# Position products of a Fourier layer, tied behind products of an output tile

## The chip, the cores and the metric

The kernel runs on one core of one Trainium2 chip. The metric is the device time of one execution in microseconds (us); three runs of the kernel before gave a median of 1564.77 us (1563.36 to 1567.52). TensorE (PE) multiplies matrices and transposes, VectorE (DVE) does elementwise work and the low parts of operands, ScalarE (ACT) copies, casts and takes activations, GpSimd (POOL) and SyncE (SP) do little but start transfers in the part of the kernel that matters here.

## The reference

Two residual layers and a final norm, on a prompt of 2048 positions and a sample of 512, 1024 channels each:

```python
def fourier_layer(x, g, w_gate, w_out):
    b, s, d = x.shape
    h = rmsnorm(x, g)
    hg = h.astype(jnp.float32).reshape(b, s, N_FGROUPS, FGROUP_CH)
    f = jnp.fft.fftn(hg, axes=(1, 3), norm="ortho").real
    f = f.reshape(b, s, d).astype(x.dtype)
    gate = h @ w_gate
    return x + (f * jax.nn.silu(gate)) @ w_out

def trunk(x, ...):
    x = attention_layer(x, ...)   # windowed attention, |i-j| <= 128
    x = fourier_layer(x, ...)
    return rmsnorm(x, final_norm)
```

The change lies in the Fourier layer, in the transform over positions of the prompt.

## The kernel before, in words

Every product of float32 matrices is made of three products of high and low parts (`matmul3`, line 131): high times high, high times low, low times high. To make the parts of an operand, ACT casts the high part and DVE subtracts it for the low part; where the text speaks of a split, it means this pair.

The Fourier layer first takes the transform over channels, tile by tile (128 positions), and combines the 16 tiles of the prompt in groups of four (`radix4`). The combined tiles ("spectra") of three groups go to DRAM (`evd`, `odd`), those of the last group stay in SBUF (`kept`). What follows runs position class by position class: `k1` from 0 to 8 stands for the output positions k1 + 16 j, and for their mirror 16 - k1 + 16 j where there is one.

For each class DVE builds one or two spectra `G[k1]` out of the loaded tiles by sums and differences (`pm`, line 2039, gives a sum in a new tile and the difference in place; `tt` is one such operation, 1024 columns, line 1502). Then `position` (line 1677) does the following. It loads the gate rows and the table of cosines and sines (`position_loads`, line 1656: SP, or POOL for mirrored rows, and POOL for the table). It takes buffers for one or two output tiles `up` with `zt`. For each half of the columns it splits the spectra (`halves_of`, line 1659: ACT L1668, DVE L1669, tiles `gp`), multiplies them by the table on PE into a pair of PSUM banks (`acc` inside `position`, tiles `ABp`: 6 products for a half of class 0 or 8, 12 for a half of the others, so 24 in each step below), and combines the two banks into `up` (ACT copies L1702 and L1705, DVE sums L1706 to L1709). At the end DVE multiplies `up` by the gate rows (L1712). PSUM has two pairs of banks for `ABp` and for the turns below.

`turned` (line 1242) transposes an `up` tile on PE (`tw`, 16 transposes, L112) and splits the result into `tTu`. `finish` (line 1745) is the output projection of such a tile: two halves of the columns, for each 8 blocks k of three products, so 48 products `fo`; DVE adds the result to the residual rows (L1759), then come the final norm (ACT L1261, DVE L127, POOL L128, DVE L1729) and the store (SP L1731).

`step` (line 1940) puts these together: the products of the new positions, the projection of the oldest waiting tile, the turns of the new tiles, the projection of the next waiting tile. The steps of the part that changes are:

- `emit(0, 8)`: classes 0 and 8, while the last two tiles of the sample (`pend`) are projected; all its spectra come from `w0`, four tiles of which three are loaded (`ev`)
- `emit(4)`: class 4, from the differences of `w0`
- `emit(2)`: class 2, from `w2`
- class 6, written out by hand: its `position`, eight loads of sums of the output weights (`f_sums("T1")`, `f_sums("T2")`, tiles `fT`), the projection of the first tile of class 2, the first half of the second tile's, the turns of class 6 (inside `o.operands`), the second half.

The order in which the engines get their work is that of a planner: each engine takes instructions from a queue in a fixed order, which the planner makes from the program's order as a priority, from its own estimate of durations, and from the buffers that are free. Tiles of one tag share a number of buffers: `right` (and so `zt`) has 16, `hT` has 8 (operands of PE), `x` has 4 (residual and gate rows). `after(ins, anchor)` (line 190) ties an instruction behind another in the queue, with no wait of its own; `matmul3` takes it as `behind`. In the kernel before, the turns are tied behind the projected tile and behind the last position product (`chain["turns"]`, `chain["B"]`), the next projection behind the turns. The position products themselves are not tied.

Of the kernel before, what the change touches and what calls it, by code (L numbers as in the profile page):

```python
# [25 lines left out]
KD = D // P  # L26
# [24 lines left out]
def f32(ap):  # L51
    return ap.bitcast(F32)
# [3 lines left out]
def encoder(  # L56
# [74 lines left out]
    def matmul3(out, a, b, start, stop, more=False, behind=None):  # L131

        for i, j in ((0, 0), (0, 1), (1, 0)):
            ins = pe(PE.matmul(out, a[i], b[j], start=start and i + j == 0, stop=stop and i == 1, skip_group_check=more))  # L134
            after(ins, behind)
        return ins
# [64 lines left out]
    def pe(ins):  # L201
        return seq(PE, ins) if PE in chain else ins
# [1013 lines left out]
    def fourier_phase(tail):  # L1216
        with ExitStack() as es:
# [9 lines left out]
            def right(shape, dtype, name):  # L1227
                return zp.tile(shape, dtype, align_bytes=LINE, tag="R", bufs=16, name=name)
# [3 lines left out]
            def zt(name):  # L1232
                return right([P, D], F32, name)
# [267 lines left out]
            def tt(out, a, b, op):  # L1501
                DVE.tensor_tensor(out, a, b, op)
# [38 lines left out]
            for i, s in enumerate(tail):  # L1541
# [7 lines left out]
                if 1 <= i < 9:  # L1549
                    w, k = split_steps[i - 1]  # L1550
# [105 lines left out]
            def position_loads(name, tab, tiles):  # L1656
                return [gated(name, r, xtile) for r in tiles], table(name, tab, left)

            def halves_of(name, gr, gs, hf, after_one=None):

                out = []
                for i, g in enumerate((gr, gs)):
                    if i and after_one:
                        after_one()
                    if g is not None:
                        t = main.tile([P, 2, 512], F32R, align_bytes=LINE, tag="hT", bufs=8, name=f"g{name}_{hf}_{i}")
                        gv = g[hf] if isinstance(g, list) else g[:, hf * 512 : hf * 512 + 512]
                        ACT.copy(t[:, 0], gv)  # L1668
                        low = DVE.tensor_tensor(t[:, 1], gv, f32(t[:, 0]), ALU.subtract)  # L1669
                        if chain.get("steps"):  # L1670
                            seq("dve", low)
                        out.append(t)
                return out
# [3 lines left out]
            def position(name, tab, gr, gs, tiles, loads=None, parts=None, between=None, later=None):  # L1677

                s2s, tb = loads or position_loads(name, tab, tiles)
                cs, sn, ns = [(tb[:, 2 * i], tb[:, 2 * i + 1]) for i in range(3)]  # L1680
                us = [zt(f"u{name}_{i}") for i in range(len(tiles))]
                for hf in range(2):
                    if hf and between:
                        between()
                    ts = parts[hf] if parts and parts[hf] else halves_of(name, gr, gs, hf)

                    def acc(out, tabs, c0, n):
                        for i, (w, t) in enumerate(zip(tabs, ts)):
                            v = [
                                t[:, part].rearrange("p (g c) -> p g c", g=2)[:, :, c0 : c0 + n]  # L1690
                                for part in range(2)
                            ]
                            end = matmul3(out, w, v, i == 0, i == len(ts) - 1)
                        return end

                    ab = two_banks(f"AB{name}_{hf}")
                    a, b = ab[:, 0, :260], ab[:, 1, :256]
                    a, b = (t.rearrange("p (g c) -> p g c", g=2) for t in (a, b))
                    chain["A"] = acc(a, (cs, ns), 0, 130)
                    chain["B"] = acc(b, (sn, cs), P, P)  # L1700
                    uv = [u.rearrange("p (g c) -> p g c", g=4)[:, 2 * hf : 2 * hf + 2] for u in us]
                    ACT.copy(uv[0][:, :, 0 : P + 1], a[:, :, 0 : P + 1])  # L1702
                    re, im = uv[0][:, :, 1:P], b[:, :, 1:P]
                    for v in uv[1:]:
                        ACT.copy(v[:, :, 0 : P + 1 : P], a[:, :, 0 : P + 1 : P])  # L1705
                        DVE.tensor_tensor(v[:, :, 1:P], re, im, ALU.add)  # L1706
                        DVE.tensor_tensor(v[:, :, P + 1 : 256], re, im, ALU.subtract)
                    DVE.tensor_tensor(uv[0][:, :, P + 1 : 256], re, im, ALU.add)
                    last_b[0] = DVE.tensor_tensor(re, re, im, ALU.subtract)  # L1709
                for u, s2 in zip(us, s2s):  # L1710
                    if later is None:
                        gated_by.append(DVE.tensor_tensor(u, u, s2, ALU.mult))  # L1712
                    else:
                        later.append(lambda u=u, s2=s2: after(DVE.tensor_tensor(u, u, s2, ALU.mult), last_c[0]))
                return list(zip(us, tiles))
# [26 lines left out]

            late = [None]

            def finish(uT, r, between=None):
                r0 = r[0]
                x2 = residual(r)
                for half in range(2):
                    if half and between:
                        chain["turns"] = end  # L1750
                        between()
                    ps = psum2.tile([P, 512], F32, tag="acc", name=f"fo{r0}_{half}")
                    for k in range(KD):
                        first_one = k == 0 and half == (between is not None)
                        end = matmul3(
                            ps, uT[k], wo[half * KD + k], k == 0, k == KD - 1, behind=chain.get("turns") if first_one else None
                        )
                    xs = x2[:, half * 512 : half * 512 + 512]
                    DVE.tensor_tensor(xs, xs, ps, ALU.add)  # L1759
# [172 lines left out]
            def pair(k1, R, base):  # L1932

                if k1 == 0 or 2 * k1 == R:
                    return [(base + k1, R, None)]
                return [(base + k1, R, None), (base + R - k1, R, k1 if R == 16 else 0)]

            pend = []

            def step(*positions):  # L1940
                new = [t for p in positions for t in position(*p)]
                if pend:
                    end = finish(*pend.pop(0))
# [70 lines left out]
            new = position(*early[0])  # L2014
# [8 lines left out]
            new = turned_one + turned(new[1:])  # L2023
# [22 lines left out]
            def emit(*ks):  # L2046
                step(*((f"p{k1}", k1, *G[k1], pair(k1, 16, 0)) for k1 in ks))

            e, g4r = pm(w0[0], w0[2], "e0")
            f, g4s = pm(w0[1], w0[3], "f0")  # L2050
            r0, r8 = pm(e, f, "r0")
            G[0], G[8], G[4] = (r0, None), (r8, None), (g4r, g4s)
            emit(0, 8)
            c2 = math.sqrt(0.5)
            sm, df = pm(w2[1], w2[3], "sm")
            g2r = zt("g2r")
# [3 lines left out]
            DVE.scalar_tensor_tensor(g2s, sm, c2, w2[2], ALU.mult, A)  # L2060
            DVE.scalar_tensor_tensor(w2[2], sm, c2, w2[2], ALU.mult, S)
            G[2], G[6] = (g2r, g2s), (w2[0], w2[2])
            emit(4)
            pc, qs = [], []
            for a in range(4):
                for i, l in enumerate((pc, qs)):
# [3 lines left out]
                    t = zt(f"od{a}_{i}")  # L2070
# [3 lines left out]
            for a in range(1, 4):  # L2074
# [6 lines left out]
                DVE.scalar_tensor_tensor(qs[a], qs[a], ca, tmp, ALU.mult, A)  # L2081
                tcs.append(c_)
                tsn.append(qs[a])
            emit(2)
            e0c, e1c = pm(tcs[0], tcs[2], "e0c")
            o0c, o1c = pm(tcs[1], tcs[3], "o0c")
            e0s, e1s = pm(tsn[0], tsn[2], "e0s")
# [15 lines left out]
            p6 = [halves_of("p6", *G[6], 0), None]  # L2103
# [5 lines left out]
            for k1 in (3, 5):  # L2109
                for t, g in zip(god[k1], G[k1]):  # L2110
                    ACT.dma_start(t, g)
            o = Outs(6, position("p6", 6, *G[6], pair(6, 16, 0), None, p6))
            f_sums("T1", right)
            f_sums("T2", right)
            finish(*pend.pop(0))
            finish(*pend.pop(0), o.operands)
            o.others()
            o.load()
# [17 lines left out]
            for k1, k2 in ((1, 7), (7, 3), (3, 5), (5, None)):  # L2136
# [30 lines left out]
                o = nxt["o"]  # L2167
# [108 lines left out]
```

## Time and profile before

| | |
|---|---|
| median of 3 runs | 1564.77 us |
| profiled execution, its own time | 1567.89 us |
| its span | 1566.1 us |
| PE busy | 1545.2 us (99%) |
| DVE busy | 1123.7 us (72%) |
| ACT busy | 889.5 us (57%) |
| POOL busy | 450.7 us (29%) |
| DMA | 237 GB/s over the span |

In a line of the timeline the columns are start and duration in us, engine, line of the program, operation, output and inputs by the program's names, shapes, and how many instructions the line merges; in brackets stands how long the engine was idle before it and what ended that. The start of a merged line is that of its first instruction. Matmuls overlap, so the durations of a group add up to a little more than the time from its start to the next group. In a table of stretches, the pairs are busy time and count for PE, PEld, DVE, ACT and POOL, then follow the granted share of TensorE's clock, the busy share of the DMA engines and GB/s. In a list of waits stand the total in us, how often, and the longest.

### The profile page before, as it was taken

Reading aid. Unit: us, or ns where it says so; the run is one execution under the profiler, and the core shown is the slowest. Engines: PE = TensorE matmul, PEld = TensorE weight load, DVE = VectorE, ACT = ScalarE, POOL = GpSimd, SP = SyncE. Lnnn points to the kernel's source line nnn. Section 1 sums busy time; section 2 is a strip of 40 time slices with the busy share of each in tenths; the row PEclk is TensorE's granted clock in tenths of the full one; section 3 lists DMA queues with packets and bytes.
Section 4 is the critical chain, followed back from the end, with each engine's and each line's share of the span. In section 5 each row is a group of like instructions: output and inputs, shape, how many; then the busy total and the mean of one; then the engine's idle time right before and its main releaser. Section 6 shows DMA issues by size and latency. Waiting matters only on the chain.

```text
span 1566.1 us, 33658 instructions
## 1 busy us (share of the span) xinstructions
PE 1545.2 (99%) x13150; PEld 1350.9 (86%) x13150; DVE 1123.7 (72%) x2431; ACT 889.5 (57%) x1921; POOL 450.7 (29%) x616
## 2 busy tenths in 40 slices
PE   9999999999999999999999999999999999899998
PEld 7899888999898888988888899988888888788886
DVE  5888655777637776367764577767888877889896
ACT  6788534787337784257861477746656554333353
POOL 2565662421414313314214142222112111101100
PEclk9999999999999999999999999999999999999999
DMA  9677687684856765866749666675666679456852
GB/s 330 232 264 234 222 336 280 216 293 161 297 218 220 243 232 204 302 210 205 251 136 363 232 206 224 243 257 181 223 234 218 220 242 409 149 202 250 298 191 94
DMA packets 100729, 372.70 MB, mean 238 GB/s; under 512 B 11235, under 2 KB 22251, under 8 KB 83420
## 3 DMA queue, kind: packets, MB, share of 16 engines
q1 hardware_dynamic: 82716, 297.38, 54.8%
q0 software_dynamic: 16688, 70.04, 11.5%
q10 hardware_dynamic: 1168, 3.15, 0.6%
q8 instruction: 103, 1.69, 0.4%
q14 instruction: 54, 0.44, 0.1%
HBM read 280.06 MB, written 90.47 MB: 237 GB/s over the span
## 4 chain that ended last, share of the span: by engine, by line
PE 88%; DVE 6%; DMA 3%; ACT 2%; issue 1%; POOL 0%; POOLq 0%; ACTq 0%; DVEq 0%; SPq 0%
PE pj L524 27%; PE av L750 7%; PE W L134 6%; PE pj L134 6%; PE tp L134 5%; PE av L134 5%; PE spt L650 5%; PE spt L134 4%; PE tp L709 3%; PE Wo L134 3%; PE fo L134 3%; PE Z L134 3%; PE z L1385 2%; PE Zo L134 2%; PE ABp L134 2%; PE X L134 1%
## 5 line engine op out<-in xcount | busy, mean ns | idle before, releaser
L524 PE MATMUL pj<-h,wg 64*128 64x512 f32 x1920 | 440.3, 390 | 0.0
L524 PE MATMUL pj<-h,wq 64*128 64x512 f32 x1560 | 380.4, 390 | 1.3 <-DVE qab L568 1.3
L524 PEld LDWEIGHTS pj<-h,wg 64*128 64x128 f32 x1920 | 331.5, 185 | 22.6
L524 PEld LDWEIGHTS pj<-h,wq 64*128 64x128 f32 x1560 | 285.4, 185 | 22.9 <-DVE qab L568 2.7
L669 DVE CUSTOM_DVE_ANT_0 S<-spt,b 128x385 f32<-128x385 f32 (+1 forms) x320 | 165.0, 525 | 94.1 <-PE spt L650 89.7
L677 ACT ACTIVATE S<-S 128x385 f32<-128x385 f32 (+1 forms) x320 | 189.2, 592 | 62.1 <-DVE S L669 40.5
L722 ACT CAST pts<-tp 128x768 fp32r<-128x768 f32 (+1 forms) x160 | 121.3, 758 | 96.6 <-PE av L750 59.8
L726 DVE TENSOR_TENSOR pts<-tp,pts 128x768 fp32r<-128x768 f32 (+1 forms) x160 | 144.1, 901 | 14.1 <-ACT pts L722 13.4
L750 PE MATMUL av<-pts,v 64*128 64x256 f32 x1680 | 143.7, 287 | 3.0 <-DVE pts L726 3.0
L750 PEld LDWEIGHTS av<-pts,v 64*128 64x128 f32 x1680 | 127.3, 186 | 7.3 <-DVE pts L726 3.8
L795 POOL TENSOR_TENSOR uT<-o,uT 128x256 fp32r<-128x256 f32 x75 | 56.7, 756 | 244.5 <-ACT uT L791 244.2
L650 PE MATMUL spt<-kwin,qab 64*128 64x384 f32 (+1 forms) x960 | 121.4, 339 | 0.9 <-DVE S L669 0.7
L134 PE MATMUL fo<-wo,tTu 128*128 128x512 f32 x480 | 115.7, 395 | 0.0
L134 PEld LDWEIGHTS fo<-wo,tTu 128*128 128x128 f32 x480 | 89.4, 190 | 18.1
L709 PEld LDWEIGHTS tp<-ident,S 64*128 64x128 f32 x1792 | 93.1, 137 | 10.1 <-DVE pts L726 3.1
L709 PE MATMUL tp<-ident,S 64*128 64x64 f32 x1792 | 98.0, 224 | 0.1
L786 POOL TENSOR_TENSOR o<-o,s 128x256 f32<-128x256 f32 x75 | 55.6, 742 | 120.3 <-DVE o L780 95.0
L692 DVE TENSOR_SCALAR S<-S 128x384 f32<-128x384 f32 (+1 forms) x192 | 88.5, 489 | 0.1
L650 PEld LDWEIGHTS spt<-kwin,qab 64*128 64x128 f32 x960 | 85.1, 188 | 3.8 <-issue 1.8
L279 DVE SCALAR_TENSOR_TENSOR h<-xk,g0s,h 128x512 fp32r<-128x512 f32 x40 | 45.3, 1146 | 51.3 <-ACT h L278 51.1
L524 PE MATMUL pj<-wo,uT 64*128 64x512 f32 x360 | 74.8, 390 | 0.0
L278 ACT ACTIVATE h<-xk,g0s 128x512 fp32r<-128x512 f32 x40 | 28.7, 724 | 75.2 <-POOL xk L274 75.1
(376 smaller groups left out, 3355.8 us busy)
## 6 DMA issues: line engine op xcount, KB each, us to landing
wo<-wsd SPq DMA_DIRECT2D x32, 1024.0 KB, 5.9
wq<-wsd SPq DMA_DIRECT2D x31, 1024.0 KB, 6.5
wg<-wsd SPq DMA_DIRECT2D x31, 1024.0 KB, 5.8
x<-x1d SPq DMA_DIRECT2D x40, 512.0 KB, 3.8
b<-b21d SPq DMA_DIRECT2D x40, 512.0 KB, 4.7
b<-rowd SPq DMA_DIRECT2D x40, 384.0 KB, 4.2
xs<-in_x_dram SPq DMA_DIRECT2D x23, 512.0 KB, 6.2
s2d<-gt POOLq DMA_DIRECT2D x40, 256.0 KB, 4.2
```

The costliest lines, as they stand in the source:

```text
L134: ins = pe(PE.matmul(out, a[i], b[j], start=start and i + j == 0, stop=stop and i == 1, skip_group_check=more))
L524: out.last[h] = pe(PE.matmul(out.ps, a[i], b[j], **out.flags()))
L650: pe(PE.matmul(spt[j][:, 2 + k0 * P : 2 + k1 * P], res["q"][rows, qp, b * P : (b + 1) * P], kwin[g][rows, kp, b * P + k0 * P : b * P + k1 ...
L669: seq(DVE, DVE.tensor_tensor_reduce(out=s[:, e0:e1], in0=ps[:, 1 + e0 : 1 + e1], in1=st["bias"][:, j, 386 - e1 : 386 - e0][:, ::-1], scale ...
L677: last_exp[0] = seq(ACT, ACT.activation(s[:, e0:e1], s[:, e0:e1], AF.Exp, bias=s[:, 386:387], scale=-1.0, accum_out=s[:, 387:388]))
L692: seq(DVE, DVE.tensor_scalar(s[:, ks], s[:, ks], den, None, ALU.mult))
L709: pe(PE.transpose(ps[h][:, kb, j, :], s[rows, j, 1 + kb * P : 1 + (kb + 1) * P], ident[rows, rows]))
L722: seq(ACT, ACT.copy(hi, ps))
L726: seq(DVE, DVE.tensor_tensor(lo, ps, f32(hi), ALU.subtract))
L750: last[i][h] = pe(PE.matmul(av[:, i, :256], v[rows], pt[rows], start=not swap and n == 0, stop=swap and n == len(todo[h]) - 1, skip_group_ ...
L786: eng.tensor_tensor(o, o, s, ALU.mult)
L795: low = eng.tensor_tensor(lo, o, f32(hi), ALU.subtract)
```

## The change

Position products can now be tied behind products of the tile that is being projected. `finish` takes a function `within` and a number `n`: after block n of its 16 (3 n products) it remembers the last product in `chain["rows"]` and calls `within`, which traces the positions; `acc` passes that product as `behind`. `step` takes the number first: 10 for classes 0 and 8 (30 products), 0 for class 4 (not tied, positions first, as before), 3 for class 2 (9 products). Before the projection starts, `step` does the loads of all its positions and the split of the first half of the first one. For class 6 the number is 10; its loads stay ahead of all, the eight loads of `f_sums` now stand ahead of its products and of its `up` tiles.

The differences of `w0` (`g4r`, `g4s`, the spectra of class 4) stood ahead of classes 0 and 8 in the program; they now stand behind that step.

```diff
-                            end = matmul3(out, w, v, i == 0, i == len(ts) - 1)
+                            end = matmul3(out, w, v, i == 0, i == len(ts) - 1, behind=chain.get("rows"))
...
-            def finish(uT, r, between=None):
+            def finish(uT, r, between=None, within=None, n=0):
...
+                        if within and half * KD + k + 1 == n:
+                            chain["rows"] = end
+                            within()
+                            chain.pop("rows")
...
-            def step(*positions):
-                new = [t for p in positions for t in position(*p)]
-                if pend:
-                    end = finish(*pend.pop(0))
+            def step(n, *positions):
+                new, held = [], []
+                for i, p in enumerate(positions):
+                    held.append((position_loads(p[0], p[1], p[4]), None if i else [halves_of(p[0], p[2], p[3], 0), None]))
+
+                def within():
+                    for p, h in zip(positions, held):
+                        new.extend(position(*p, *h))
+
+                if not n:
+                    within()
+                end = finish(*pend.pop(0), None, within, n)
...
-            e, g4r = pm(w0[0], w0[2], "e0")
-            f, g4s = pm(w0[1], w0[3], "f0")
+            e, f = zt("e0"), zt("f0")
+            for n, a, b in ((e, 0, 2), (f, 1, 3)):
+                tt(n, w0[a], w0[b], A)
             r0, r8 = pm(e, f, "r0")
-            G[0], G[8], G[4] = (r0, None), (r8, None), (g4r, g4s)
-            emit(0, 8)
+            G[0], G[8], G[4] = (r0, None), (r8, None), (w0[0], w0[1])
+            emit(10, 0, 8)
+            for a in range(2):
+                tt(w0[a], w0[a], w0[a + 2], S)
...
-            emit(4)
+            emit(0, 4)
...
-            emit(2)
+            emit(3, 2)
...
-            o = Outs(6, position("p6", 6, *G[6], pair(6, 16, 0), None, p6))
+            six = []
+            at6 = position_loads("p6", 6, pair(6, 16, 0))
             f_sums("T1", right)
             f_sums("T2", right)
-            finish(*pend.pop(0))
+            finish(
+                *pend.pop(0), None,
+                lambda: six.append(Outs(6, position("p6", 6, *G[6], pair(6, 16, 0), at6, p6))), 10,
+            )
+            o = six[0]
             finish(*pend.pop(0), o.operands)
```

More of the change, by code (lines that the diff above doesn't have):

```diff
@@ L2044, in pm, with emit @@
                 return n, a
-            def emit(*ks):
-                step(*((f"p{k1}", k1, *G[k1], pair(k1, 16, 0)) for k1 in ks))
-            e, g4r = pm(w0[0], w0[2], "e0")
-            f, g4s = pm(w0[1], w0[3], "f0")
+            def emit(n, *ks):
+                step(n, *((f"p{k1}", k1, *G[k1], pair(k1, 16, 0)) for k1 in ks))
+            e, f = zt("e0"), zt("f0")
+            for n, a, b in ((e, 0, 2), (f, 1, 3)):
+                tt(n, w0[a], w0[b], A)
             r0, r8 = pm(e, f, "r0")
-            G[0], G[8], G[4] = (r0, None), (r8, None), (g4r, g4s)
-            emit(0, 8)
+            G[0], G[8], G[4] = (r0, None), (r8, None), (w0[0], w0[1])
+            emit(10, 0, 8)
+            for a in range(2):
+                tt(w0[a], w0[a], w0[a + 2], S)
             c2 = math.sqrt(0.5)
```

## The prediction

> **What bounds the kernel now.** I read the page's busy times, then TensorE's waits late in the run, then granted clock and busy times by stretch, then the timeline of TensorE and of the engines that feed it.
>
> ```profile
> span 1566.1 us, 33658 instructions
> ...
> PE 1545.2 (99%) x13150; PEld 1350.9 (86%) x13150; DVE 1123.7 (72%) x2431; ACT 889.5 (57%) x1921; POOL 450.7 (29%) x616
> ```
>
> TensorE (PE) is the bound: 20.9 us of the span are not PE. No product is added or removed, so the change can only move waits of PE. From 1318 to 1450 us, where all edits lie, the waits are:
>
> ```profile
> PE ABp L134 <- ACT gp L1668: 4.3, 1, 4.3
> ...
> PE ABp L134 <- DVE gp L1669: 1.0, 2, 0.8
> ```
>
> and the stretches around the long one (PE, PEld, DVE, ACT, POOL busy; PEclk is the granted clock):
>
> ```profile
> 1334.37:1338.70 4.33, 0.00 (x1) 0.00 (x0) 4.33 (x7) 0.67 (x2) 0.00 (x0) 0.79 0.41 146
> 1338.70:1346.00 7.30, 7.30 (x28) 6.30 (x29) 5.30 (x10) 3.31 (x7) 1.45 (x2) 0.66 0.39 136
> ```
>
> PE stands for 4.33 us, and afterwards runs at 0.66 of its clock for 7.30 us, which costs another 7.30 x 0.34 = 2.5 us. VectorE (DVE) is the cause: it is busy for all 4.33 us of the gap. PE's queue, in order of time:
>
> ```profile
> 1325.47 8.90 PE L134 MATMUL fo<-wo,tTu 128*128 128x512 f32 x38
> 1338.70 0.58 PE L134 MATMUL ABp<-gp,tbp 128*128 128x260 f32 x1 [4.33 <-ACT gp L1668]
> ...
> 1354.08 1.21 PE L112 MATMUL tw<-ident,up 64*128 64x64 f32 x32
> 1355.22 11.19 PE L134 MATMUL fo<-wo,tTu 128*128 128x512 f32 x48
> 1366.25 3.06 PE L134 MATMUL ABp<-gp,tbp 128*128 128x260 f32 x24
> ...
> 1394.49 2.57 PE L134 MATMUL ABp<-gp,tbp 128*128 128x260 f32 x19 [0.24 <-DVE gp L1669]
> ...
> 1418.92 0.41 PE L134 MATMUL ABp<-gp,tbp 128*128 128x260 f32 x2
> ...
> 1425.15 0.63 PE L134 MATMUL ABp<-gp,tbp 128*128 128x260 f32 x3 [0.79 <-DVE gp L1669]
> ...
> 1439.41 1.21 PE L112 MATMUL tw<-ident,up 64*128 64x64 f32 x32
> ```
>
> An output tile is 48 `fo` products in 11.03 us (1355.22 to 1366.25), 0.23 us each; 24 position products take 2.89 us (from the row's start plus 3.06, less the overlap), 0.12 each.
>
> **The change, part by part.**
>
> *First step (positions 0 and 8, behind 30 products).* Of the 38 products at 1325.47, 34 finish the tile before; so the step's tile starts at 1325.47 + 34 x 0.23 = 1333.3, and only 4 of its products stand ahead of the waiting `ABp`. Behind 30, `ABp` comes at 1333.3 + 6.9 = 1340.2, after the 1338.70 at which its operand is there today. The gap and the slow clock go: +6.8 us at most.
>
> What is late next is DVE. Its rows, with the ScalarE (ACT) copy that first writes `up` of position 8:
>
> ```profile
> 1328.03 1.23 DVE L1502 TENSOR_TENSOR e<-ev,ev 128x1024 f32<-128x1024 f32 x1 [4.37 <-DMA ev<-evd]
> ...
> 1329.77 1.22 DVE L1502 TENSOR_TENSOR ev<-ev,ev 128x1024 f32<-128x1024 f32 x1
> ...
> 1335.65 1.22 DVE L1502 TENSOR_TENSOR ev<-ev,z 128x1024 f32<-128x1024 f32 x1
> ...
> 1341.46 1.28 DVE L1729 SCALAR_TENSOR_TENSOR x<-x,invf,gfb 128x1024 f32<-128x1024 f32 x1 [0.45 <-POOL invf L128]
> ...
> 1344.01 0.42 DVE L1708 TENSOR_TENSOR up<-up,ABp 128x254 f32<-128x254 f32 x1 [1.27 <-ACT up L1702]
> ...
> 1345.06 0.74 DVE L1709 TENSOR_TENSOR up<-up,ABp 128x254 f32<-128x254 f32 x2
> 1345.72 0.69 DVE L1669 TENSOR_TENSOR gp<-e,gp 128x512 fp32r<-128x512 f32 x1
> ...
> 1347.68 0.38 ACT L1702 COPY up<-ABp 128x258 f32<-128x258 f32 x1 [2.99 <-PE ABp L134]
> ...
> 1350.17 1.22 DVE L1502 TENSOR_TENSOR sm<-ev,er 128x1024 f32<-128x1024 f32 x1
> ...
> 1352.77 1.22 DVE L1712 TENSOR_TENSOR up<-up,s2p 128x1024 f32<-128x1024 f32 x1
> ```
>
> DVE started late: it stood idle for 4.37 us until the spectra `ev` had landed. The two differences (`ev<-ev` at 1329.77, 1335.65) leave the way of `r`, which comes up to 2.3 us sooner. But the planner fills a free DVE with whatever is ready, and while it waits for 26 more products the differences and position 8's two splits (0.69 each) are ready. So ahead of the first `up` sum stands the work that ends at 1342.74 today, differences included, plus two splits: about 1344.0. PE's first 12 `ABp` end at 1340.2 + 1.45 = 1341.65. Position 8 can start only when three `up` sums (two take 0.74 at 1345.06) have emptied one of the two PSUM pairs: 1344.0 + 1.1 and 0.1 of latency = 1345.2. The planner, which takes DVE to be in time, puts some five `fo` products there, until 1342.8. New wait: 2.4 us. Bounds: none, if the differences fall behind the sums; 4.3 us, if DVE is as late as now. I take 2.4, the sum of rows.
>
> Does a 2.4 us wait cost clock? By the row, 0.79 over 4.33 us is half rate for 1.8 us, so the drop came 2.5 us into the gap; I charge 0.6 us, a quarter of 2.5, bounds 0 and 2.5. [...]
>
> From there PE has 12 `ABp` (1.45 us) and some 13 `fo` products (3.0) up to the turns `tw`; DVE has four more sums (1.5) and two products of `up` (1.22 each, as at 1352.77), 3.9 us. So the turns wait for nothing that counts.
>
> *Second step (position 4, not tied).* The differences must now precede its splits, and `sm` (1350.17) moves behind the turns too, because of the buffers (below). That puts up to 2.3 us more on DVE before 1366.25 less the shift; the tile's own products fill in. Cost 0 to 1.5, taken 0.5.
>
> *Third step (position 2, behind 9).* Its `ABp` come 9 x 0.23 = 2.1 us into the tile instead of at its head: the 0.24 us wait goes. +0.2, nothing behind it is short.
>
> *Position 6 (behind 30), and the loads.* The rows are SyncE's loads, the landing of the `ev` loads among them, and DVE's work:
>
> ```profile
> 1310.11 9.07 SPq L2034 DMA_DIRECT2D ev<-evd  x6
> ...
> 1427.49 3.22 SPq L1929 DMA_DIRECT2D fT<-fT1d  x4
> ...
> 1432.33 8.86 SPq L1929 DMA_DIRECT2D fT<-fT2d  x4
> ```
>
> ```profile
> ev<-evd SPq DMA_DIRECT2D x6, 512.0 KB, 14.0
> ```
>
> ```profile
> 1429.09 1.22 DVE L1502 TENSOR_TENSOR g5s<-tc,od 128x1024 f32<-128x1024 f32 x1
> ...
> 1431.95 0.41 DVE L1706 TENSOR_TENSOR up<-up,ABp 128x254 f32<-128x254 f32 x1
> ...
> 1437.25 1.23 DVE L1712 TENSOR_TENSOR up<-up,s2p 128x1024 f32<-128x1024 f32 x1
> ...
> 1440.12 0.68 DVE L1759 TENSOR_TENSOR x<-x,fo 128x512 f32<-128x512 f32 x1
> ```
>
> Its `ABp` come at 1418.92 + 6.9 = 1425.8, after 1425.15: the 0.79 us wait goes, +0.8. But `f_sums("T1")` and `("T2")`, eight SyncE loads into the 16 buffers of `right`, now stand ahead of position 6's two `up` tiles, which take buffers of the same tag. The planner gives a tag's buffers in program order, each at the tile's first write. The rows bear it out: `sm`'s inputs are of six loads, the last issued by 1319.2 (1310.11 + 9.07) and 14.0 us to landing, so there by 1333.2; DVE was idle for 1.27 us before 1344.01; yet `sm`, the tag's next tile after position 8's `up`, ran only behind the first write of that `up` at 1347.68. So the copies into position 6's `up` are planned after the eighth load, and the loads after `g5s`, the tag's tile before them.
>
> Six such loads took 9.07 us, so eight from 1429.09 end near 1441. By then PE has done the 42 products that follow `ABp` (18 of this tile, 24 of the next; 9.7 us), and the add of that next half tile (1440.12 today, behind all of `up`) is ready, so it is planned ahead of the `up` sums. DVE works in the order of its queue: the sums, which begin at 1431.95 today, would wait for PE's 42nd product. Then come the add (0.6), eight sums (0.74 for two, 3.0) and two products (2.3, less their overlap), with latency 5.8 us, in which PE stands before `tw`: the other 24 products are ordered behind the turns. That gap is longer than the one whose slow clock cost 2.5, so 2.5 again: -8.3. Bounds: 0, if the sums stay ahead of the add; -9.2, since half rate lasted 1.8 + 7.30 x 0.68 = 6.8 us in all, and costs 3.4 if every bit of it falls on busy PE.
>
> The loads' own time, position 6's rows and table (SyncE and POOL; ahead of the loads as before), and the pre-split of position 0's first half (already the first work of the step) cost nothing: none of it is among what PE waits for in the rows above.
>
> Sum: 6.8 - 2.4 - 0.6 - 0.5 + 0.2 + 0.8 - 8.3 = -4.0, i.e. 4.0 us slower. The profiled execution took 1567.89 us (1566.1 span, 1.8 around it), 3.1 over the median 1564.77, so it would be 1571.9; on the median, 1568.8.
>
> **The rivals.**
>
> *No new wait at position 6.* The `up` sums stay ahead of the add, because buffers are given otherwise than I read. For: today's margin is there, last product at 1437.25, turns at 1439.41. Against: `sm`'s row. Time: 6.8 - 2.4 - 0.6 - 0.5 + 0.2 + 0.8 = 4.3 faster, 1560.5; with no new wait in the first step 7.3 faster, 1557.5. This is the case on the other side, and it decides at one point: whether the first write of position 6's `up` is queued before that add.
>
> *The first wait only moves.* DVE, late by the landing of `ev`, makes PE stand at position 8 as long as it stands now, clock drop included. For: DVE is busy through the whole gap. Against: the 1.27 us that it idled before 1344.01. With the wait at position 6: 6.8 - 6.8 - 0.5 + 1.0 - 8.3 = -7.8: 1572.6.
>
> *It does nothing.* The first wait moves as in the case before, and position 6 stays whole: 6.8 - 6.8 - 0.5 + 1.0 = 0.5 faster, 1564.3. For and against as above.
>
> **How the numbers follow.** 0.3%, 4.7 us, is about what a measurement of this kernel can tell from no change. Chances: my forecast 0.40, no wait at position 6 0.36, wait moved with position 6 late 0.16, nothing 0.08. The forecast's own range, from the bounds of its terms, is 1565.3 (6.8 + 1.0 - 8.3) to 1574.5 (6.8 - 4.3 - 2.5 - 1.5 + 1.0 - 9.2); three fifths of it I put within 4.7 us, the rest slower. Half of the second case passes 4.7 us, most of the third is slower by more, and the last is hardly ever either. So faster 0.18 + 0.02 = 0.20, same 0.24 + 0.18 + 0.03 + 0.06 = 0.51, slower 0.16 + 0.13 = 0.29. The range 1558.8 to 1572.8 leaves out the best fifth of the second case and the worst tail of the third.
>
> **What would show it.** Right: no wait of `ABp` on `gp` near 1338, granted clock 1.00 there, a PE wait of 2 to 3 us before position 8's first `ABp`, turns near 1350; `fT2` all issued before the first copy to position 6's `up`; `tw` waiting near 6 us for an `up` product, clock below 1 behind it. Wrong: `tw` at position 6 without a wait, or position 8 without one.

## The result, and the profile after

| | median, us | ratio to the kernel before, 95% interval |
|---|---|---|
| before, 7 runs | 1564.77 (1563.16 to 1567.52) | |
| after, 7 runs | 1572.22 (1570.35 to 1573.49) | 1.0041 (1.0030 to 1.0052) |

The change makes the kernel 7.45 us slower. The profiled execution of after took 1573.49 us (span 1571.7). Its page has the same work as before:

```profile
span 1571.7 us, 33660 instructions
...
PE 1545.0 (98%) x13150; PEld 1350.3 (86%) x13150; DVE 1123.6 (71%) x2431; ACT 890.8 (57%) x1921; POOL 452.0 (29%) x616
```

PE's busy time is 1545.0 against 1545.2 us, so the 5.6 us by which the spans differ are waits. (PE counts as busy at a low clock too, only for longer: the 32 turns take 1.97 us at a granted clock of 0.50, at 1443.52 below, and 1.21 us at 1.00, at 1350.73. What the low clock costs is about the same in both executions, as the last section shows.) The waits of PE from 1318 to 1450 us:

```profile
PE tw L112 <- DVE up L1712: 7.0, 1, 7.0
PE ABp L134 <- issue: 2.2, 1, 2.2
PE ABp L134 <- DVE gp L1669: 0.6, 2, 0.4
```

The 4.3 us wait on ACT's cast of `gp` is gone. In its place stand 2.2 us in the first step ("issue": the profile names no engine that ended this wait), and 7.0 us in front of the turns of class 6. The stretches of these two waits and of what follows them (columns as in the table of stretches before):

```profile
1342.05:1344.29 2.24, 0.00 (x1) 0.03 (x1) 2.21 (x5) 0.00 (x0) 0.00 (x0) 1.00 0.67 179
1344.29:1350.73 6.44, 6.44 (x27) 5.30 (x27) 5.55 (x9) 0.76 (x2) 0.00 (x0) 0.74 0.71 239
1436.54:1443.52 6.98, 0.01 (x2) 0.04 (x2) 6.79 (x12) 0.00 (x0) 0.00 (x0) 0.79 1.05 416
1443.52:1451.90 8.38, 8.38 (x57) 7.07 (x57) 5.18 (x8) 4.69 (x9) 0.00 (x0) 0.77 0.86 310
```

In both waits DVE is busy nearly throughout (2.21 of 2.24, 6.79 of 6.98). Both are followed by a low granted clock: 6.44 x 0.26 = 1.7 us lost behind the first, 8.38 x 0.23 = 1.9 behind the second.

PE's queue in order of time; the residual add is L1763 in this kernel (L1759 before), the loads of `f_sums` are L1933 (L1929):

```profile
1324.86 14.80 PE L134 MATMUL fo<-wo,tTu 128*128 128x512 f32 x64
1339.50 1.61 PE L134 MATMUL ABp<-gp,tbp 128*128 128x260 f32 x12
1340.95 1.10 PE L134 MATMUL fo<-wo,tTu 128*128 128x512 f32 x4
1344.29 2.46 PE L134 MATMUL ABp<-gp,tbp 128*128 128x260 f32 x12 [2.24 <-issue]
1346.55 4.25 PE L134 MATMUL fo<-wo,tTu 128*128 128x512 f32 x14
1350.73 1.21 PE L112 MATMUL tw<-ident,up 64*128 64x64 f32 x32
...
1422.42 2.12 PE L134 MATMUL ABp<-gp,tbp 128*128 128x260 f32 x13
1424.94 0.63 PE L134 MATMUL ABp<-gp,tbp 128*128 128x260 f32 x3 [0.40 <-DVE gp L1669]
1425.41 1.09 PE L134 MATMUL fo<-wo,tTu 128*128 128x512 f32 x4
1426.68 1.23 PE L134 MATMUL ABp<-gp,tbp 128*128 128x260 f32 x8 [0.18 <-DVE gp L1669]
1427.74 8.80 PE L134 MATMUL fo<-wo,tTu 128*128 128x512 f32 x38
1443.52 1.97 PE L112 MATMUL tw<-ident,up 64*128 64x64 f32 x32 [6.97 <-DVE up L1712]
```

Cut at the turns, the span divides so:

| stretch | before | after | difference |
|---|---|---|---|
| up to the row of products that ends the last tile and begins the first step's | 1325.47 | 1324.86 | -0.6 |
| from there to the turns of the first step | 28.61 | 25.87 | -2.7 |
| to the turns of class 6 | 85.33 | 92.79 | +7.5 |
| to the end | 126.69 | 128.18 | +1.5 |
| span | 1566.1 | 1571.7 | +5.6 |

The first step gains 2.7 us, class 6 and the slow clock behind it lose 9. DVE's timeline shows what its queue does at class 6:

```profile
1433.10 0.15 DVE L127 TENSOR_SCALAR invf<-ssf 128x1 f32<-128x1 f32 x1 [1.27 <-ACT jkf L1261]
1436.58 0.69 DVE L1763 TENSOR_TENSOR x<-x,fo 128x512 f32<-128x512 f32 x1 [3.33 <-PE fo L134]
1437.19 0.41 DVE L1706 TENSOR_TENSOR up<-up,ABp 128x254 f32<-128x254 f32 x1
...
1439.49 1.22 DVE L1712 TENSOR_TENSOR up<-up,s2p 128x1024 f32<-128x1024 f32 x1
1440.62 0.41 DVE L1709 TENSOR_TENSOR up<-up,ABp 128x254 f32<-128x254 f32 x1
1440.95 1.28 DVE L1729 SCALAR_TENSOR_TENSOR x<-x,invf,gfb 128x1024 f32<-128x1024 f32 x1
1442.15 1.22 DVE L1712 TENSOR_TENSOR up<-up,s2p 128x1024 f32<-128x1024 f32 x1
```

Just before the turns' wait DVE stands idle for 3.33 us, because the head of its queue is the add of the next half tile, which waits for PE's 42nd product. The `up` sums stand behind it, then the two products of `up` with a norm's scale (L1729) between them; then PE may turn. The first of ACT's copies into `up` had run long before, while SyncE was still issuing the second four loads:

```profile
1432.97 0.36 ACT L1702 COPY up<-ABp 128x258 f32<-128x258 f32 x1
```

```profile
1429.52 8.60 SPq L1933 DMA_DIRECT2D fT<-fT2d  x4
```

### The profile page after: what moved, and what is told of

Its sections match the earlier page's. It is cut to its first block, busy times and chain, and to the rows that moved or that the text cites. A ratio compares the mean times of both kernels' runs of the same rounds, so it can differ in the third digit from the quotient of the medians.

```text
span 1571.7 us, 33660 instructions
## 1 busy us (share of the span) xinstructions
PE 1545.0 (98%) x13150; PEld 1350.3 (86%) x13150; DVE 1123.6 (71%) x2431; ACT 890.8 (57%) x1921; POOL 452.0 (29%) x616
## 4 chain that ended last, share of the span: by engine, by line
PE 88%; DVE 5%; issue 3%; ACT 2%; DMA 1%; POOL 1%; SPq 0%; POOLq 0%; DVEq 0%; ACTq 0%
PE pj L524 27%; PE av L750 7%; PE W L134 6%; PE tp L134 5%; PE spt L650 5%; PE pj L134 5%; PE av L134 5%; PE fo L134 5%; PE spt L134 4%; PE tp L709 3%; PE Wo L134 3%; PE Z L134 3%; PE z L1385 2%; PE Zo L134 2%; PE X L134 1%
```

## The experiments

Two theories of the loss: the order of the loads against the `up` tiles of class 6 makes it (forecast), or the tie does, by bringing the position products late. All kernels below were timed against the kernel before on the same chip, and the ratios are to those runs.

**Loads back behind position 6.** After, with `f_sums` moved into the function that traces position 6:

```diff
-            f_sums("T1", right)
-            f_sums("T2", right)
...
+            def six_products():
+                six.append(Outs(6, position("p6", 6, *G[6], pair(6, 16, 0), at6, p6)))
+                f_sums("T1", right)
+                f_sums("T2", right)
...
```

> The changed kernel with one thing put back: the eight weight loads of class 6 stand behind its position again in the program, so its two up tiles take their buffers first; ties and differences stay as changed. Buffer-order theory: the 6.97 us wait of tw for an up product goes, and the half-rate clock behind it (0.77 over 8.38 us, 1.9 us); left are the first step's gain (turns 2.7 us sooner after the row at 1325.47) and small waits. 1572.2 - 7.5 - 1.5 = about 1563, 1 to 3 us under the kernel before. Rival, the tie behind 30 products makes class 6 late by itself: the wait stays at 5 us or more and the time at 1569 or above.

1562.23 us, ratio 0.9994 (0.9983 to 1.0005): by the ratio 0.9 us under the kernel before, where 1 to 3 were expected. The turns of class 6 wait for nothing:

```profile
1423.40 8.80 PE L134 MATMUL fo<-wo,tTu 128*128 128x512 f32 x38
1432.13 1.21 PE L112 MATMUL tw<-ident,up 64*128 64x64 f32 x32
```

The tie of class 6 is still there, so the tie alone doesn't make the wait.

**Class 6 alone.** Before, with the class 6 edits (loads ahead, tie behind 30 products) and nothing else.

> The kernel before with the edits of class 6 alone (loads ahead, products behind 30): no tie in the three steps, differences where they were. Buffer-order theory: the whole loss without the first step's gain, so the 4.33 us wait near 1338 stays and tw of class 6 waits some 6 to 7 us: 1564.8 + 7.5 + 1.5 = about 1573.5. Rival, the loss comes from the steps before running ahead of DVE: tw of class 6 waits under 2 us and the time is 1564 to 1567.

1574.55 us, ratio 1.0059 (1.0041 to 1.0077); the turns wait 6.97 us.

**Loads ahead alone.** Before, with `f_sums` ahead of position 6 and no tie anywhere:

```diff
-            o = Outs(6, position("p6", 6, *G[6], pair(6, 16, 0), None, p6))
+            at6 = position_loads("p6", 6, pair(6, 16, 0))
             f_sums("T1", right)
             f_sums("T2", right)
+            o = Outs(6, position("p6", 6, *G[6], pair(6, 16, 0), at6, p6))
```

> The kernel before with the eight weight loads ahead of class 6's position in the program and nothing else: its products are not tied. Buffer-order theory: the copies into up still come behind the eighth load and the sums behind the add of the next tile's first half, so tw waits some 6 to 7 us as in the changed kernel: about 1573, within 1.5 us of class 6 changed as a whole. Rival, the tie is what costs: no wait at tw, 1564 to 1566.

1571.66 us, ratio 1.0053 (1.0036 to 1.0070), and the same wait to the hundredth:

```profile
1440.60 1.97 PE L112 MATMUL tw<-ident,up 64*128 64x64 f32 x32 [6.97 <-DVE up L1712]
```

The order of the loads alone, without a tie, makes the whole loss. The second theory falls.

**Steps alone.** After, with class 6 as before.

> The changed kernel with class 6 entirely as before (not tied, loads behind): the three ties and the moved differences alone. Theory: the first step's gain alone, 4.33 and 2.5 us against a new wait of 2.2 us and 1.7 us of slow clock, less what the second step costs: 1 to 3 us under the kernel before, 1562 to 1564. Against the kernel with only the loads put back it tells what the tie of class 6 does by itself: up to 0.8 us for the tie if DVE keeps up, nothing if DVE is the limit there. Rival, the gain of the first step is lost by class 2, where DVE is the limit: no difference from the kernel before.

1562.65 us, ratio 0.9990 (0.9980 to 1.0000): by the ratio the steps gain 1.6 us, with an interval from 0 to 3.1. Class 6 tied (1562.23) or not (1562.65) makes no difference that can be seen.

**The add behind the `up` products.** What remained open was how the loads do it: do they hold the buffers until they have landed, or do they only set the order in which DVE's queue was planned? After, with one order more:

```diff
-                    DVE.tensor_tensor(xs, xs, ps, ALU.add)
+                    add = DVE.tensor_tensor(xs, xs, ps, ALU.add)
+                    if not half:
+                        after(add, chain.pop("up", None))
...
             o = six[0]
+            chain["up"] = gated_by[-1]
```

> The changed kernel, eight loads still ahead of position 6's up tiles, with one order more: the add of the next half tile (the one that waits for PE's 42nd product) stands on DVE behind position 6's last up product. Theory A (the loads delay only the planned order; the wait of 6.97 us is made by that add in front of the up sums): the sums start with the copies into up, near 1433.4 instead of 1437.19, 3.8 us sooner, so tw waits 3.2 us instead of 6.97; time 1567 to 1569. Theory B (the buffers themselves come late, because the loads hold them): the sums stay near 1437, the wait near 6.4 (only the add's 0.6 us leaves the way), time 1571 to 1573.

1567.02 us, ratio 1.0015 (1.0006 to 1.0023). DVE, then PE:

```profile
1433.46 0.42 DVE L1706 TENSOR_TENSOR up<-up,ABp 128x254 f32<-128x254 f32 x1 [0.17 <-ACT up L1705]
...
1439.57 0.68 DVE L1763 TENSOR_TENSOR x<-x,fo 128x512 f32<-128x512 f32 x1
```

```profile
1439.79 1.97 PE L112 MATMUL tw<-ident,up 64*128 64x64 f32 x32 [3.21 <-DVE up L1712]
```

With all eight loads where the change put them, the sums start at 1433.46 instead of 1437.19, and the wait is 3.21 us (3.2 expected). The buffers were there; the add at the head of DVE's queue was the wait. What is left is the chain itself: from 1433.46 the sums, L1729 and the two products take 6.2 us, while PE's 42 products end at 1436.58.

**Four loads ahead, four behind.**

```diff
             f_sums("T1", right)
-            f_sums("T2", right)
...
+            def six_products():
+                six.append(Outs(6, position("p6", 6, *G[6], pair(6, 16, 0), at6, p6)))
+                f_sums("T2", right)
...
```

> The changed kernel with four of the eight loads ahead of position 6's up tiles (T1) and four behind (T2). Theory A (the buffers go out in program order, so the copies into up are planned after the last load that stands ahead): with four loads the sums are planned some 4 us sooner, ahead of the add that waits for PE's 42nd product; only the last up product stays behind that add; wait of tw 1.9 us (0.69 for the add, 1.22 for the product) instead of 6.97, time 1563 to 1566. Theory B (any load ahead of up makes the wait): near 7 us and 1571 or more.

1565.20 us, ratio 1.0006 (0.9996 to 1.0017). DVE, then PE:

```profile
1430.66 0.41 DVE L1706 TENSOR_TENSOR up<-up,ABp 128x254 f32<-128x254 f32 x1
...
1435.49 0.69 DVE L1763 TENSOR_TENSOR x<-x,fo 128x512 f32<-128x512 f32 x1 [0.92 <-PE fo L134]
1436.09 1.28 DVE L1712 TENSOR_TENSOR up<-up,s2p 128x1024 f32<-128x1024 f32 x1
```

```profile
1437.52 1.21 PE L112 MATMUL tw<-ident,up 64*128 64x64 f32 x32 [2.07 <-DVE up L1712]
```

The sums now stand ahead of the add, and only the last product is behind it: 2.07 us (1.9 expected). With none, four and eight loads ahead of the `up` tiles the turns wait 0, 2.07 and 6.97 us. So the length of that row of loads sets how far the sums slip back in DVE's queue, as buffers handed out in program order would have it.

The next kernels look at the first step, whose gain was smaller than forecast. They compare one quantity, the lateness L: the start of `e` on DVE (which waits for `ev`) less the start of PE's row of products.

**Tie alone.** After with the loads back, and the differences of `w0` ahead of `r` as before.

> The changed kernel with the eight loads back behind position 6, but with the two spectra differences where they stood before (ahead of r), so that of the first step only the tie is left. Lateness L: start of e less start of the 38 to 64 output products in which the first step lies. In the traces so far the wait in the order of before was 1.77 + L (L 2.56, 1.09, -0.28; waits 4.33, 2.85, 1.49), and behind 30 products 0.20 + L (L 2.04, 2.46; waits 2.24, 2.66; L -1.05, no wait). Theory A (DVE's whole work ahead of the first up sum sets the wait, whatever its order): the differences ahead of r change nothing, wait in front of position 8 of L - 0.3 to L + 0.2, none in front of position 0 for L under 2; time as with the loads back, 1561 to 1563.5. Theory B (the differences must leave the way of r for the tie to work): a wait in front of position 0 too, time 2 us or more above it.

1563.01 us, ratio 0.9997 (0.9987 to 1.0007); a wait of 1.77 us in front of position 8, none in front of position 0. With the tie, the moved differences bought nothing: the work ahead of the first `up` sum is the same, in whatever order.

**Sums first.** After with the loads back, and the two differences ordered behind position 8's `up` product:

```diff
-                tt(w0[a], w0[a], w0[a + 2], S)
+                after(DVE.tensor_tensor(w0[a], w0[a], w0[a + 2], S), gated_by[-1])
```

> The changed kernel with the eight loads back behind position 6, and with the two differences ordered on DVE behind position 8's last up product. Theory A (what DVE has queued ahead of the first up sum makes PE stand in front of position 8): 2.3 us less ahead of the sums, so the wait is L - 2.1, i.e. none for L under 2; with L as in the traces so far (-1 to 2.6, mean 1.1) the time is 1 to 2.5 us under that with the loads back, 1559.5 to 1561.5. Theory B (the wait is not DVE's order but the landing of ev): wait 0.2 + L as before, time unchanged near 1562. Against both: the differences, now late, make position 4's splits late; then ABp waits near 1366 on gp by 0.5 to 2 us and nothing is gained.

1562.58 us, ratio 0.9991 (0.9981 to 1.0000). No wait in the first step, and DVE now idles in front of the first sum:

```profile
1340.68 0.42 DVE L1708 TENSOR_TENSOR up<-up,ABp 128x254 f32<-128x254 f32 x1 [1.01 <-ACT up L1702]
```

L was only 0.25 in this execution, where the tie with the differences would have waited 0.45 us: the idle DVE shows the slack, but the time can't be told from that of the kernel with the loads back (ratio 0.9994), where 1 to 2.5 us less were expected. Class 2 gives 0.55 us back (a new wait of `ABp` on DVE's L127).

**`ev` in two groups of three.** After with the loads back; the three `ev` loads that `e` and `f` need first, the others behind `r`'s first write. And the same in the kernel before, with nothing else:

```diff
...
+            def ev_loads(i, l):
...
+            ev_loads(0, w0)
...
+            ev_loads(1, w2)
             emit(10, 0, 8)
```

> The changed kernel with the eight loads back behind position 6, and with the six ev loads in two groups of three: the three that e and f need first, the other three behind the first write of r. Theory A (L is set by six loads of 512 KB landing together, about 13 us each): three land sooner, L falls by 3 us or more, below -1, no wait in front of position 8 and clock 1.00; time 1 to 2 us under that with the loads back, near 1560.5. Theory B (L is set by when the buffers or the queue let the loads start): L stays -1 to 2.6, wait and time as with six. Against: sm waits for the late three, DVE stands near 1343 and the turns of position 8 come late.

1561.95 us, ratio 0.9992 (0.9983 to 1.0001), L 0.26, wait 0.46 us; the 1 to 2 us under the kernel with the loads back that were expected do not show.

> The kernel before, with only the six ev loads in two groups of three. Theory A (the 4.33 us in front of position 0 are the late landing, 1.77 + L): L near -3, no wait, clock 1.00, time 2 to 4 us under before, 1560 to 1562, i.e. no less than the ties gain. Theory B (DVE's work between e and the splits bounds it, whatever the landing): wait stays above 1.5 us and the time at 1563 to 1564.

1563.98 us, ratio 1.0003 (0.9994 to 1.0012), L -0.84. The wait is down to 0.92 us and the span to 1559.5, but the median time is that of the kernel before. The expected gain of 2 to 4 us was missed. The profiled execution is no measure of this kernel: its span is the shortest of eleven, whose median is 1562.2, against 1562.5 for the 33 executions of the kernel before. L did not fall by 3 us either: in the first of the two kernels the three loads are issued by 1311.83 and `e` starts at 1324.06, 12.2 us later. Counted from where the issue of the third load ends, `e` starts 11.1 to 12.2 us later in the three kernels with groups of three (the candidate below is one of them), and 11.0 to 13.9 us later in the eleven with six. The DMA engines are full with three loads (1.03 and 1.08 below) as they are with six (1.02 and 1.05 in the kernel before):

```profile
1312.00:1318.00 6.00, 6.00 (x43) 4.84 (x42) 6.00 (x11) 3.42 (x7) 0.57 (x2) 1.00 1.03 398
1318.00:1324.00 6.00, 6.00 (x41) 4.76 (x40) 3.96 (x7) 1.71 (x4) 1.56 (x3) 1.00 1.08 410
```

So the three loads that were taken away did not hold up the first three; that those stand behind a backlog of other transfers is likely, but not shown.

**Differences alone.** Before, with the differences behind the first step and no tie.

> The kernel before, with the two spectra differences behind the first step and no tie. L as in the runs so far (start of e less start of the row of products), and 1.77 + L the wait in the order of before. The split of r is then 2.3 us less behind e, but four more output products are no longer in front of position 0. Theory A (DVE's work between e and the first splits sets the wait): wait in front of position 0 of L + 1.2 or less, 0.5 us or more under before at the same L; a second wait in front of position 8 up to 1 us; time within 1 us of before. Theory B (only the tie shortens the first step): wait 1.77 + L as before, time as before or more.

1564.19 us, ratio 0.9998 (0.9989 to 1.0006); L 1.55 and a wait of 2.92 us, where the order of before would have waited 3.32. They help by 0.4 us, a little less than the 0.5 expected: DVE's split comes sooner, but four `fo` products fewer stand in front, 4 x 0.23 = 0.9 us.

**Both, as a candidate.** Groups of three and sums first, loads back.

> Candidate for a version that beats both: the changed kernel with the eight loads behind position 6, the ev loads in two groups of three, and the two differences on DVE behind position 8's up product. Theory A (first step freed of every wait for L under 2; class 6 without the wait): no wait from position 0 to the turns; 1561 to 1562.5, 0.1 to 0.2% under before. Theory B (what the first step saves is given back at position 4 and 2, where the late differences make splits late): waits of 0.5 to 1 us there, 1562.5 to 1563.5.

1562.46 us, ratio 0.9990 (0.9981 to 0.9999): no wait from position 0 to the turns, as the first theory has it, and 0.55 us given back in class 2, as the second has it. It beats both kernels, the one before by 0.1%, about what the interval can tell.

L and the wait of the first step, from the timelines of twelve of the fourteen profiled executions (in the two others, with the sums first, there is no wait, at L of 0.25 and -0.81):

| order of the first step | L and wait, us | wait less L |
|---|---|---|
| before | 2.56, 4.33; 1.09, 2.85; -0.28, 1.49; -0.84, 0.92 | 1.76 to 1.77 |
| tied behind 30 | 2.46, 2.66; 2.55, 2.74; 2.04, 2.24; 1.62, 1.81; 1.56, 1.77; 0.26, 0.46; -1.05, none | 0.19 to 0.21 |
| differences behind, no tie | 1.55, 2.92 | 1.37 |

For one row of it, the kernel before with `ev` in groups: `e` on DVE, then PE.

```profile
1323.49 1.23 DVE L1502 TENSOR_TENSOR e<-ev,ev 128x1024 f32<-128x1024 f32 x1 [0.93 <-DMA ev<-evd]
```

```profile
1324.33 8.91 PE L134 MATMUL fo<-wo,tTu 128*128 128x512 f32 x38
1334.16 0.39 PE L134 MATMUL ABp<-gp,tbp 128*128 128x260 f32 x1 [0.92 <-ACT gp L1668]
```

The wait is L and a constant of the order of work. The tie behind 30 products, 6 us of PE's time, takes 1.57 us off it. L itself differs between executions, from -1.05 to 2.56; the three with groups of three have 0.26, -0.81 and -0.84, low in that range, and whether that is chance three executions can't tell.

## Why the prediction was right or wrong

It forecast 1568.8 us, with a sum of 4.0 us against; the time is 1572.22, inside its range of 1558.8 to 1572.8 and near its end. It gave the larger chance (0.51) to a change within 0.3%; measured is 0.41% slower (0.30 to 0.52), a case to which it gave 0.29. The rival with the first wait moved whole names 1572.6 us, which is nearer, but by luck: that wait did not move whole, as shown below. The rivals without a new wait at class 6 are out by the 6.97 us there.

*Class 6: right in its mechanism, too small in one term.* The tag's buffers in program order, the sums planned behind the eighth load, the add of the next half tile ahead of them, the turns behind the sums: the two experiments with loads ahead show the place, the one with the add behind shows the link. One sign named for it was wrong: `fT2` was not all issued before the first copy to `up` (1432.97, the loads ran on to 1438.1). The planned order is what counted, not when the loads really ran. The forecast wait of 5.8 us measured 6.97. The missing 1.2 us are the norm's scale L1729, which the planner put between the two `up` products (1440.95 to 1442.15). The term for the slow clock, 2.5, was 1.9 here, and 1.8 and 2.9 with the loads ahead alone and with class 6 alone.

*Class 6's position products.* Forecast was +0.8 us, for the wait at 1425.15 before. After has waits of 0.40 and 0.18 there, and the 13 products at 1422.42 take 2.12 us where 13 x 0.12 = 1.6 were to be expected. Nothing was gained that can be seen: behind 30 products DVE's splits are still late.

*First step: the wait was right, its clock and its worth were not.* No wait on `gp` near 1338, a wait of 2.24 us in front of position 8 (2.4 forecast), turns at 1350.73 (near 1350 forecast). The rival in which the wait moves whole is out: 1.57 us less at the same L. DVE's rows in front of that wait's end (PE goes on at 1344.29):

```profile
1342.73 0.68 DVE L1763 TENSOR_TENSOR x<-x,fo 128x512 f32<-128x512 f32 x1
1343.32 0.41 DVE L1708 TENSOR_TENSOR up<-up,ABp 128x254 f32<-128x254 f32 x1
1343.77 0.42 DVE L1709 TENSOR_TENSOR up<-up,ABp 128x254 f32<-128x254 f32 x1
```

PE goes on 0.1 us after the second `up` sum, so two sums are enough and not the three of the forecast. On the other side, an add that the forecast did not count stands ahead of them. That 2.24 came so near 2.4 is partly luck: `ev` landed 0.5 us sooner against PE's row than in the execution from which the forecast was read (L 2.04, not 2.56); at 2.56 the table's 0.20 + L would give 2.76. And the clock behind the new wait cost 1.7 us and not the 0.6 charged. The forecast took the drop to come 2.5 us into a wait, as it did in before; here it came 0.69 us behind the wait's end, at 1344.98, and lasted 3.41 us, all of them on busy PE (last section). So 6.8 - 2.4 - 0.6 = 3.8 us in the forecast stand against 2.7 measured from profile to profile.

*From the profile to the median.* Stage by stage, the forecast was 3.8 - 5.3 - 2.5 = -4.0 and the profiles show 2.74 - 7.46 - 1.49 = -6.2; after was 0.6 us ahead when the first step began, which is not the change's doing, and 5.6 remain. The medians differ by 7.45, because the profiled execution of before was 3.1 us above its median and that of after only 1.3 above. Two things made that execution of before long: L at 2.56, and a stretch at half rate from 91.01 to 94.42, 3.41 x 0.5 = 1.7 us, that after does not have (its granted clock is 1.00 from 87 to 95). The step that failed is the last sentence of the sum: it carried 6.8 us, read in an execution with L at 2.56, over to a median execution. Eleven executions with six `ev` loads together have L from -1.05 to 2.56, mean 1.30. Steps alone gained 1.6 us by the time.

*Second and third step.* The second, charged at 0.5, shows no wait. The 0.24 us wait of the third is gone in after, as forecast.

*What the steps are worth.* At the mean L of 1.30 the table gives 3.07 us of wait before and 1.50 tied; by the two profiles' prices a clock loss of 1.7 us would go as well, some 3 us in all. The ratios of the tied kernels without the loads give 0.5 to 1.6 us (0.9997 to 0.9990). Two parts of the difference show in the runs. Behind class 6 some is given back: from those turns to the end the tied kernels take 127.0 to 127.4 us against 126.7 before, and five of the six show a new wait there of 0.2 to 0.5 us, of `Wo` products on DVE. And the clock gains less: over all executions, the granted clocks and spans give 3.1 to 3.3 us lost before and 1.9 to 2.3 in these six kernels, 0.8 to 1.2 us less. So an estimate from these figures is 1.6 of wait, 0.8 to 1.2 of clock, less 0.3 to 0.7: 1.7 to 2.5 us. The intervals of the ratios reach 2.0 to 3.1 us on the faster side, so what is left is hardly more than the noise; it stays open.

## What to carry to other kernels

Where a planner hands out buffers in program order, moving a few loads ahead of a tile that shares their tag moves that tile's whole work back in every queue, even if nothing needs the loads yet and the buffers are free: look for what then stands at the head of the slower engine's queue and whom it waits for. Before pricing a wait as gain, see in several executions whether it is there in all of them: here the lateness of one load made it anything from 0.9 to 4.3 us. Work taken off the way of one engine is worth only the distance to the next thing that is late: 6 us of postponed products took 1.6 us off the wait.

## What the runs showed of the hardware

The low clock comes in stretches. While PE has work, before has one of 3.41 us at half rate (from 91.01) and one of 6.83 us (from 1336.87), after one of 3.41 us (from 1344.98) and one of 6.83 us (from 1440.56). In the kernel with class 6 alone the granted clock is 0.69 over the 7.00 us of its long wait and 0.66 over the 8.70 us behind it, so 5.1 us are lost there, or some 10.3 us at half rate.

Within one execution the starts lie whole multiples of 3.413 us apart: in after 1344.98 and 1440.56, 28 x 3.413, and 1566.85, behind the last product, 37 x 3.413 later; in before 1336.87 and 1562.15, 66 x 3.413. Against the waits they lie differently: 2.50 us into the 4.33 us wait of before, 4.0 us into the 6.97 us wait of after, and 0.69 us behind the end of its 2.24 us wait. The 3.41 us ahead of such a start and the 3.41 us from it, in before:

```profile
1333.46:1336.87 3.41, 0.91 (x5) 0.41 (x3) 3.41 (x5) 0.00 (x0) 0.00 (x0) 1.00 0.41 169
1336.87:1340.28 3.41, 1.58 (x5) 1.38 (x6) 3.41 (x5) 2.25 (x5) 0.00 (x0) 0.50 0.48 147
```

In after:

```profile
1341.57:1344.98 3.41, 1.17 (x9) 0.76 (x7) 3.34 (x6) 0.00 (x0) 0.46 (x1) 1.00 0.65 203
1344.98:1348.40 3.42, 3.42 (x14) 2.99 (x13) 2.75 (x6) 0.76 (x2) 0.00 (x0) 0.50 0.52 120
```

Two pairs of the kernel with four loads ahead, the second at the start of a stretch and the first 27 x 3.413 us earlier:

```profile
1343.09:1346.51 3.42, 1.79 (x13) 1.77 (x14) 3.32 (x7) 0.38 (x1) 0.00 (x0) 1.00 0.86 262
1346.51:1349.92 3.41, 3.41 (x23) 2.56 (x23) 3.41 (x7) 0.38 (x1) 0.00 (x0) 1.00 0.43 106
1435.26:1438.67 3.41, 1.34 (x34) 1.11 (x33) 3.08 (x3) 0.40 (x1) 1.54 (x3) 1.00 1.03 420
1438.67:1442.09 3.42, 3.42 (x10) 2.74 (x9) 3.17 (x6) 2.31 (x5) 0.00 (x0) 0.50 1.06 406
```

In these pairs half rate follows 2.50, 2.24 and 2.07 us of idle PE, and the full clock follows 1.63. With four loads ahead the wait of 1.81 us runs from 1342.91 to 1344.72, so that 1.63 us of it lie behind 1343.09; the wait of 2.07 us, from 1435.45 to 1437.52, lies whole in the 3.41 us ahead of 1438.67. By whole waits, from 1318 to 1450 us: those of 2.07, 2.24, 2.66, 2.74, 2.85, 2.92, 3.21, 4.33 and 6.97 us had half rate in them or behind them, those of 0.46, 0.92, 1.49, 1.77 and 1.81 us had the full clock. Lengths between 1.81 and 2.07 us did not occur, and whether the whole wait counts or its part in such a piece of 3.41 us, no run shows.

The length does not tell it alone. At 88.01 us of the kernel before, in another part of the program, PE waits 1.39 us for DVE, and from 91.01 the clock is at half rate. After has a wait of 1.39 us at the same place, from 88.56, and a granted clock of 1.00 from 87 to 95. What else counts stays open.

The price follows from where a stretch falls. Behind each of the waits of 2.07, 2.24, 2.66, 2.74, 2.85, 2.92 and 3.21 us it is 1.6 to 1.7 us, what one stretch of 3.41 us at half rate costs that falls on busy PE nearly whole (in after PE is busy from 1344.98 to 1348.40 throughout). Behind the 4.33 us wait it was 2.5, behind those of 6.97 us 1.8 to 2.9: there the clock falls within the wait, and stays low for 6.83 us in before and in after. So the two executions compared here lost about as much to the clock in all: before 1.7 + 2.5 us, after 1.7 + 1.9. Near 2 us a little less waiting was worth much more than its own length here: with four loads ahead 1.81 us cost no clock, 2.07 us cost 1.7.
